# Three rebuilt weight sums fetched from DRAM scratch, row-scale sums on ScalarE, and a new loop order in a two-level seven-product matmul

## The chip, the cores and the metric

The kernel runs on one core of one Trainium2 chip. The metric is the time of one execution in device microseconds (us). Three runs of the kernel before took 1449.6, 1449.54 and 1449.25 us; the median is 1449.54 us. The engines are named PE (TensorE matmul), PEld (its weight loads), DVE (VectorE), ACT (ScalarE), POOL (GpSimd) and SP (SyncE, which here issues every transfer of the steady loop).

## The reference

```python
x: (8, 2048, 2048) float32      w: (2048, 2048) float32
cs   = np.cumsum(x, axis=1)
diff = cs - np.concatenate([zeros, cs[:, :-1, :]], axis=1)
out  = np.matmul(diff, w).astype(np.float32)
```

The difference of a running sum is x again, so the kernel computes out = x w: 16384 rows of 2048, in 128 tiles of 128 rows.

## The kernel before, in words

**Two levels of seven products.** w lies in on-chip memory as float16 in four blocks with the sums T1 to T4 beside them. The first four row tiles are multiplied plainly while w arrives, the next groups have passages of their own, and from then on a loop works through groups of four tiles, called g, h, k, l. The pair (g, k) and the pair (h, l) each are a 2 x 2 block problem, and the outer level needs seven products P1 to P7 for it. P6 and P7 are done whole: four pieces each for g and for h, with four matmuls in a piece (`P6g.0` to `P7h.3`). P1 to P5 join g and h once more into an inner 2 x 2 problem with seven quarter products, `p1` to `p7`, of four matmuls each. So a group has 5 x 7 + 16 = 51 steps of four matmuls, 204 in all, each 128 x 128 by 128 x 512.

**The weight sums.** A quarter product needs a sum of weight quarters. Most are kept. Six have no room and are rebuilt for every group into one buffer, `flow` (128 x 2048 float16, 512 KB): the sums for P1.p4, P2.p4, P3.p2, P4.p4, P5.p5 and P5.p4. Each is one subtraction or addition on DVE (`fill_by`, L955; steps named `P1.fp4` and so on). As `flow` is one buffer, a fill can begin only when the product that read the last content is over. (In the last group P4's sum goes to another buffer.)

**The rows.** A tile of x comes in as two loads of 512 KB (`load`, L113) into the buffer F, which has three places for the first half of a tile and two for the second. ACT sums the absolute values of each half (`weigh0`, `weigh1`, L125); DVE adds the two sums and takes the reciprocal (`scale`, L142 and L144); POOL makes the factors for the way back (`unit`, L150); ACT scales the rows to float16 in place (`narrow0`, `narrow1`, L164); two transfers transpose them (`turn0`, `turn1`, L177). The products go to the eight PSUM banks; ACT copies (`keep`, L636; `P1.cg`, `P5.cg` and the like, L1046) and DVE adds (`add`, L639; L1053) bring them into results of 128 x 512, which SP stores (`put`, L650).

**What sets the order.** `ORDER` is a list of step names written out by hand. A step marked +0 is of one group, +1 of the next, +2 of the one after. The list is gone through once per group, and `after(engine, ...)` makes every instruction of an engine issue after the one before it in this list, so each engine, and SP with its transfers, works strictly in list order: an instruction that waits holds back everything behind it on its engine. Loads, transposes and stores all stand in the one list of SP. `END_ORDER` and `SOONER` reorder the last group. There are 30 groups of this kind; the first of them has its own order for all but P4 and C21.

Of the kernel before, what the change touches and what calls it, by code (L numbers as in the profile page):

```python
# [10 lines left out]
def kernel(  # L11
# [34 lines left out]
    END = M // P  # L46
# [57 lines left out]
    unit = {}  # L104
# [13 lines left out]
    def weigh(t, sides=range(2)):  # L118
        if t < END:
            if t not in sums_of:  # L120
                sums_of[t] = numbers.tile([P, 8], f32, name="of")
            for i in sides:
                after(
                    "act",
                    lambda: nc.scalar.activation(  # L125
                        waste,
                        where[t][i],
                        ABS,
                        scale=1.0 / ROW,
                        accum_out=sums_of[t][:, i : i + 1],  # L130
                    ),
                )

    def scale_of(t):
        if t < END:
            m2 = sums_of.pop(t)
            m, s = (m2[:, i : i + 1] for i in (2, 3))
            u = m2[:, 4:6]
            scales[t], unit[t] = s, u
            after(  # L140
                "dve",
                lambda: nc.vector.tensor_scalar(m, m2[:, :1], m2[:, 1:2], TINY, ADD, MAX),  # L142
            )
            after("dve", lambda: nc.vector.reciprocal(s, m))  # L144
            sizes[t] = m
# [40 lines left out]
    with ExitStack() as head:  # L186
# [195 lines left out]
        for ko in range(1, KO - 1):  # L382
# [3 lines left out]
            q = (ko + 1) // KQ  # L386
# [192 lines left out]
    def in_twos(t):  # L579
        return t if len(t.shape) == 4 else t.rearrange("p (a b) n -> p a b n", b=2)  # L580
# [371 lines left out]
    def fill_by(op, a, b):  # L952
        def some(to):
            x, y = (in_twos(t) for t in (a, b))
            after("dve", lambda: nc.vector.tensor_tensor(in_twos(to), x, y, op))  # L955

        return some

    sevens = {
        "P1": (in_1, {"p4": fill_by(SUB, quarter_of(0, 1, 0), S1_all)}),  # L960
        "P2": (in_2, {"p4": fill_by(SUB, quarter_of(4, 1, 0), inner[:, 8:12, :])}),
        "P3": (in_3, {"p2": fill_by(ADD, spare_of(2, 0), inner[:, 16:20, :])}),
        "P4": (in_4, {"p4": fill_by(SUB, quarter_of(7, 1, 0), spare_of(2, 4))}),
        "P5": (
            in_5,
            {
# [6 lines left out]
    scratch = list(passing)  # L973

    class Group:
        def __init__(self, g):
            self.tiles = dict(g=g, h=g + 2, k=g + 1, l=g + 3)
            self.last = g + 4 == END
            self.at = {}
            self.do = {}  # L980
            self.sums = {}
            self.plan()
# [57 lines left out]
                p1=a[0], p2=a[1], p3=to[4], p4=b[1], p5=to[1], p6=to[2], p7=to[3]  # L1040
            )

        def copy(self, name, to, pool, b):
            def some():
                c, p = self.take(to, pool), self.at[b]
                after("act", lambda: nc.scalar.copy(c, p))  # L1046
# [24 lines left out]

# [24 lines left out]
        def plan(self):  # L1096
            tiles = self.tiles
            half = {}
# [76 lines left out]
            self.add("C12h1", q, "q")  # L1175
            self.add("C12h0", q, "q", let=True)

            self.whole("P7", T3, half["g"][0], half["h"][0], *x)
            for n, c in zip(x, ("C22h0", "C22h1", "C22g0", "C22g1")):
                self.add(c, n, "x")  # L1180

# [48 lines left out]
                    self.step(f"{P}{c}.{j}", some, a, to, j)  # L1230

    ORDER = """
    put.C12g1+0 turn1.h+1 add.C12h1.q+0 P4.p6+0 P4.p5+0 P1.cg+1 P1.p2+1
    add.C12h0.q+0 put.C12h0+0 P1.s1+1 narrow1.k+1 P4.s4+0 P4.p3+0 turn0.k+1
    keep.C21g1+0 P1.s2+1 P1.s4+1 P1.p5+1 add.C22h0.x+0 P1.ct+1 add.C21h1.e+0
    unit.h+1 P1.p6+1 unit.g+1 add.C21g1.q+0 add.C21g0.x+0 weigh0.l+1 P1.s3+1
    weigh1.l+1 turn1.k+1 P2.cv+1 P4.p4+0 add.C21g1.x+0 put.C12h1+0 put.C21g1+0
    P1.m1+1 P4.p7+0 P1.fp4+1 put.C21g0+0 load.g+2 P2.s1+1 P2.s2+1 P1.p7+1
    P1.m2+1 P2.s4+1 P2.p1+1 P1.p3+1 keep.C11g1+1 S1.g+1 S2.g+1 P1.p4+1
    keep.C11g0+1 add.C21h1.q+0 scale.l+1 unit.l+1 narrow0.l+1 put.C22h0+0  # L1240
    put.C21h1+0 P2.p2+1 add.C11g0.v+1 P6g.0+1 P2.fp4+1 P2.p6+1 turn0.l+1
    narrow1.l+1 turn1.l+1 keep.C11h1+1 P6g.1+1 P2.s3+1 add.C11g1.q+1 unit.k+1
    S4.g+1 P2.p5+1 P6g.3+1 keep.C11h0+1 add.C11h1.e+1 P2.p7+1 keep.C21h0+0
    add.C11h1.q+1 P6g.2+1 weigh0.g+2 load.h+2 add.C21h0.x+0 P5.p1+1 P2.p4+1
    S3.g+1 keep.C12g1+1 P2.p3+1 keep.C12g0+1 add.C11h0.q+1 put.C11h0+1 P5.fp5+1
    weigh1.g+2 S1.h+1 P7g.0+1 P5.s1+1 P7g.1+1 scale.g+2 P5.cg+1 P5.s2+1 P5.s4+1
    put.C21h0+0 narrow0.g+2 narrow1.g+2 S2.h+1 P5.s3+1 P5.p2+1 P5.p5+1 P5.ct+1
    add.C11g1.e+1 P5.fp4+1 P5.p6+1 P5.m1+1 put.C11g0+1 keep.C22g0+1 weigh0.h+2
    weigh1.h+2 S4.h+1 P3.s1+1 put.C11h1+1 P6h.2+1 P6h.1+1 put.C11g1+1 P3.s2+1
    P6h.3+1 P6h.0+1 keep.C12h1+1 P5.p7+1 P5.m2+1 keep.C22h1+1 S3.h+1 P3.s4+1  # L1250
    P3.s3+1 P7g.2+1 P7g.3+1 P5.p4+1 add.C22g0.x+1 P3.fp2+1 P5.p3+1 keep.C12h0+1
    add.C12h1.z+1 P7h.0+1 load.k+2 P3.p2+1 scale.h+2 narrow0.h+2 P3.p1+1 P7h.2+1
    put.C22g0+1 turn0.g+2 turn1.g+2 add.C12g0.z+1 weigh0.k+2 add.C12g0.q+1
    put.C12g0+1 P4.fp4+1 keep.C22g1+1 P7h.1+1 P7h.3+1 add.C22g1.x+1 put.C22g1+1
    P3.p3+1 add.C22h1.x+1 P4.s1+1 P4.s3+1 put.C22h1+1 keep.C22h0+1 P3.p6+1
    P3.p4+1 add.C12g1.q+1 add.C12g1.z+1 turn0.h+2 add.C12h0.z+1 weigh1.k+2
    narrow1.h+2 load.l+2 P3.p5+1 scale.k+2 P4.p2+1 P4.p1+1 keep.C21g0+1
    keep.C21h1+1 P3.p7+1 narrow0.k+2 P1.p1+2 add.C12g1.e+1 add.C12h1.e+1 P4.s2+1
    """
    ORDER = [(s[:-2], int(s[-2:])) for s in ORDER.split()]  # L1260
    early = max(n for _, n in ORDER)
# [26 lines left out]
    for b in range(-early, len(groups) - late):  # L1288
        for name, ahead in ORDER:
            i = b + ahead  # L1290
            if 0 <= i < len(groups) and name in groups[i].do:
                if i == len(groups) - 1 and name in END_ORDER:
                    continue
                if groups[i] is half and name == 'keep.C21h1':
                    continue
                if i == 1 and name in before:
                    before[name]()
                groups[i].do.pop(name)()
                if groups[i] is first and name == 'P1.cg':
# [36 lines left out]
```

## Time and profile before

| | |
|---|---|
| median of three runs | 1449.54 us |
| profiled execution, first to last instruction | 1447.4 us |
| PE busy | 1437.9 us (99%) |
| DVE busy | 1319.0 us (91%) |
| ACT busy | 970.5 us (67%) |
| POOL busy | 43.8 us (3%) |
| transfers' packets, share of 16 DMA engines | 86.5% |
| granted TensorE clock | 1.000 |

The profile describes one execution. For that execution only the span is listed, no time of its own beside it, and the span is 2.1 us less than the median of the runs. Busy shares are means over the whole span; matmuls are pipelined and their ends are modelled. A time "to landing" of a transfer runs from the start of its issue on SP to its completion semaphore.

### The profile page before, as it was taken

What the parts mean: (1) busy time and instruction counts of PE and PEld (TensorE: products, weight loads), DVE (VectorE), ACT (ScalarE), POOL (GpSimd) and SP (SyncE); (2) the same over time, 40 slices, a digit from 0 to 9 for tenths busy, and PEclk for the clock granted to TensorE, in tenths of its full rate; (3) what the DMA queues carried; (4) which work ended last, traced back from release to release, by engine and by line L of the source; (5) the groups of instructions that cost most, each with busy time, mean ns of one, the idle gap of its engine ahead of it and who ended that gap; (6) DMA issues with size and microseconds to landing.
All of it is one profiled execution on the core that took longest, in us unless ns stands there. A gap on an engine that the chain in (4) does not pass through costs nothing.

```text
span 1447.4 us, 20191 instructions
## 1 busy us (share of the span) xinstructions
PE 1437.9 (99%) x6686; PEld 651.6 (45%) x6692; DVE 1319.0 (91%) x2310; ACT 970.5 (67%) x1472; POOL 43.8 (3%) x130
## 2 busy tenths in 40 slices
PE   8999999999999999999999999999999999999998
PEld 4444444444444444444444444444444444444443
DVE  4899899999999999999999999999999999999998
ACT  6987566666666776666666667666667766666662
POOL 0011000000000000000000000000000000000000
PEclk9999999999999999999999999999999999999999
DMA  9999788899888898888899888998878998889973
GB/s 363 368 257 298 200 234 232 239 253 253 226 224 239 238 254 245 231 233 236 248 247 232 234 238 233 262 240 234 228 234 240 252 234 239 226 242 248 255 200 127
DMA packets 378199, 351.58 MB, mean 243 GB/s; under 512 B 274800, under 2 KB 274800, under 8 KB 377968
## 3 DMA queue, kind: packets, MB, share of 16 engines
q1 hardware_dynamic: 378096, 350.31, 86.5%
q8 instruction: 52, 0.85, 0.2%
q14 instruction: 51, 0.42, 0.1%
HBM read 150.99 MB, written 134.22 MB: 197 GB/s over the span
## 4 chain that ended last, share of the span: by engine, by line
PE 97%; DMA 2%; DVE 0%; SPq 0%; issue 0%; DVEq 0%
PE b L628 62%; PE b L609 33%; PE b L304 2%; DMA W<-in_w_dram 2%; DMA W<-in_x_dram 0%; DVE c L639 0%; PE b L464 0%; SPq L225 0%; DVE wb L267 0%; SPq L259 0%; DVEq L267 0%; DVEq L639 0%
## 5 line engine op out<-in xcount | busy, mean ns | idle before, releaser
L639 DVE SCALAR_TENSOR_TENSOR c<-b,of,c 128x512 f32<-128x512 f32 x790 | 573.6, 746 | 71.1 <-PE b L628 61.4
L609 PE MATMUL b<-W,x 128*128 128x512 f16 x2144 | 507.1, 379 | 0.0
L636 ACT ACTIVATE c<-b,of 128x512 f32<-128x512 f32 x492 | 312.7, 680 | 220.2 <-PE b L628 113.8
L628 PE MATMUL b<-W,x 128*128 128x512 f16 x1904 | 454.9, 379 | 0.0
L164 ACT ACTIVATE F<-F,of 128x1024 f16<-128x1024 f32 x246 | 282.3, 1148 | 175.6 <-DVE of L144 173.4
L628 PEld LDWEIGHTS <-x 128*128 128x128 f16 x2500 | 244.6, 98 | 295.4 <-issue 1.0
L609 PEld LDWEIGHTS <-x 128*128 128x128 f16 x2144 | 209.7, 98 | 253.3 <-issue 0.5
L125 ACT ACTIVATE waste<-F 128x1024 uint8<-128x1024 f32 x246 | 259.3, 1054 | 8.3 <-DMA F<-in_x_dram 6.2
L628 PEld LDWEIGHTS <-inner 128*128 128x128 f16 x1644 | 160.8, 98 | 194.0
L628 PE MATMUL b<-W,inner 128*128 128x512 f16 x940 | 241.2, 379 | 0.0
L599 DVE TENSOR_TENSOR x<-x,x 128x1024 f16<-128x1024 f16 (+1 forms) x390 | 227.1, 583 | 3.3
L628 PE MATMUL b<-flow,x 128*128 128x512 f16 x584 | 149.9, 379 | 0.0
L628 PE MATMUL b<-inner 128*128 128x512 f16 x472 | 121.1, 379 | 0.0
L955 DVE TENSOR_TENSOR flow<-W 128x2048 f16<-128x2048 f16 x87 | 105.7, 1215 | 0.0
L1053 DVE TENSOR_TENSOR b<-b,c 128x512 f32<-128x512 f32 x116 | 80.4, 693 | 12.7 <-PE b L628 12.7
L150 POOL TENSOR_SCALAR of<-uw,of 128x2 f32<-128x2 f32 x124 | 42.6, 357 | 1299.6 <-DVE of L142 717.1
L955 DVE TENSOR_TENSOR flow<-W,inner 128x2048 f16<-128x2048 f16 x58 | 70.7, 1220 | 0.0
L1046 ACT COPY c<-b 128x512 f32<-128x512 f32 x58 | 33.4, 576 | 51.2 <-PE b L628 51.2
L304 PE MATMUL b<-wb,xP 128*128 128x512 bf16 x234 | 53.2, 379 | 2.2 <-ACT wb L265 1.1
L599 DVE TENSOR_TENSOR inner<-x 128x512 f16<-128x512 f16 x117 | 49.3, 421 | 3.1 <-DMA x<-F 1.0
L1046 ACT COPY b<-b 128x512 f32<-128x512 f32 x87 | 51.2, 589 | 0.2 <-PE b L628 0.2
L599 DVE TENSOR_TENSOR inner<-x,inner 128x512 f16<-128x512 f16 x117 | 49.2, 421 | 2.0
(68 smaller groups left out, 517.5 us busy)
## 6 DMA issues: line engine op xcount, KB each, us to landing
F<-in_x_dram SPq DMA_DIRECT2D x246, 512.0 KB, 5.2
out_dram<-c SPq DMA_DIRECT2D x492, 256.0 KB, 3.0
W<-in_w_dram SPq DMA_DIRECT2D x32, 512.0 KB, 8.4
W<-in_x_dram SPq DMA_DIRECT2D x16, 256.0 KB, 7.8
x<-F SPq DMA_TRANSPOSE x246, 3.4
out_dram<-o SPq DMA_DIRECT2D x5, 256.0 KB, 7.0
out_dram<-wb SPq DMA_DIRECT2D x5, 256.0 KB, 7.0
xP<-in_x_dram SPq DMA_DIRECT2D x1, 1024.0 KB, 6.4
```

The lines of the kernel that those rows point to most:

```text
L125: lambda: nc.scalar.activation(waste, where[t][i], ABS, scale=1.0 / ROW, accum_out=sums_of[t][:, i : i + 1],),
L150: after("pool", lambda: nc.gpsimd.tensor_scalar(u, uw, m, None, MUL))
L164: lambda: nc.scalar.activation(narrowed(t)[:, ds(i * NH, NH)], where[t][i], COPY, scale=s),
L304: lambda: nc.tensor.matmul(ps[r][n], xP[:, r, ko, :], wb[h, ko][:, ds(n * NB, NB)], start=(ko == 0), stop=(ko == KO - 1),),
L599: after("dve", lambda: nc.vector.tensor_tensor(dst.all, p.all, q.all, op))
L609: said = nc.tensor.matmul(to[n], a[k], b[k][:, n, :], start=(first and k == 0), stop=(k == KH - 1), skip_group_check=True,)
L628: said = nc.tensor.matmul(to, a[k], b[k], start=(first and k == 0), stop=(k == 3), skip_group_check=True)
L636: after("act", lambda: nc.scalar.activation(c, p, COPY, scale=u))
L639: after("dve", lambda: nc.vector.scalar_tensor_tensor(c, p, u, c, MUL, ADD))
L955: after("dve", lambda: nc.vector.tensor_tensor(in_twos(to), x, y, op))
L1046: after("act", lambda: nc.scalar.copy(c, p))
L1053: after("dve", lambda: nc.vector.tensor_tensor(t, p, s, ADD))
```

## The change

Four things are edited.

1. `kept_from` wraps three of the six fills: P1.fp4, P3.fp2 and P4.fp4. The first time, the DVE instruction fills the buffer as before, and SP stores the 512 KB to a DRAM tile. Every later time SP fetches the 512 KB from that tile into the buffer, and DVE does nothing. The other three fills stay on DVE.
2. The two absolute sums of a row are added on ACT (`activation` Identity with the second sum as bias) instead of on DVE (L142). The guard against zero, which was a maximum in the DVE instruction, becomes a bias of TINY / 2048 in each element of the absolute sum (L125). The reciprocal stays on DVE.
3. `ORDER` is a new permutation of the same 188 steps.
4. `Group` takes a flag `fine` with a new method `seven_more`, which would do P7 by seven quarter products. Every group is made with `fine` False, so nothing of it is issued. `SOONER` skips a step that is already done.

```diff
                         ABS,
+                        bias=TINY / D,
                         scale=1.0 / ROW,
...
             after(
-                "dve",
-                lambda: nc.vector.tensor_scalar(m, m2[:, :1], m2[:, 1:2], TINY, ADD, MAX),
+                "act",
+                lambda: nc.scalar.activation(m, m2[:, :1], IDENTITY, bias=m2[:, 1:2]),
             )
             after("dve", lambda: nc.vector.reciprocal(s, m))
...
+    kept = ctx.enter_context(
+        tc.tile_pool(name="kept", bufs=1, space=bass.MemoryType.DRAM)
+    )
+
+    def kept_from(make, name):
+        home = kept.tile([P, 4 * NB], f16, name=name)
+        known = []
+
+        def some(to):
+            flat = in_twos(to).rearrange("p a b n -> p (a b n)")
+            if known:
+                after("sp", lambda: nc.sync.dma_start(flat, home))
+            else:
+                make(to)
+                after("sp", lambda: nc.sync.dma_start(home, flat))
+                known.append(True)
+
+        return some
+
     sevens = {
-        "P1": (in_1, {"p4": fill_by(SUB, quarter_of(0, 1, 0), S1_all)}),
+        "P1": (in_1, {"p4": kept_from(fill_by(SUB, quarter_of(0, 1, 0), S1_all), "P1p4")}),
         "P2": (in_2, {"p4": fill_by(SUB, quarter_of(4, 1, 0), inner[:, 8:12, :])}),
-        "P3": (in_3, {"p2": fill_by(ADD, spare_of(2, 0), inner[:, 16:20, :])}),
-        "P4": (in_4, {"p4": fill_by(SUB, quarter_of(7, 1, 0), spare_of(2, 4))}),
+        "P3": (in_3, {"p2": kept_from(fill_by(ADD, spare_of(2, 0), inner[:, 16:20, :]), "P3p2")}),
+        "P4": (in_4, {"p4": kept_from(fill_by(SUB, quarter_of(7, 1, 0), spare_of(2, 4)), "P4p4")}),
...
-            self.whole("P7", T3, half["g"][0], half["h"][0], *x)
+            if self.fine:
+                self.small_sums("P7", A("g", 0), A("h", 0), True, {2: A("l", 0)[0]})
+                self.seven_more("P7", *x)
+            else:
+                self.whole("P7", T3, half["g"][0], half["h"][0], *x)
...
     ORDER = """
-    put.C12g1+0 turn1.h+1 add.C12h1.q+0 P4.p6+0 P4.p5+0 P1.cg+1 P1.p2+1
...
-    unit.h+1 P1.p6+1 unit.g+1 add.C21g1.q+0 add.C21g0.x+0 weigh0.l+1 P1.s3+1
-    weigh1.l+1 turn1.k+1 P2.cv+1 P4.p4+0 add.C21g1.x+0 put.C12h1+0 put.C21g1+0
-    P1.m1+1 P4.p7+0 P1.fp4+1 put.C21g0+0 load.g+2 P2.s1+1 P2.s2+1 P1.p7+1
-    P1.m2+1 P2.s4+1 P2.p1+1 P1.p3+1 keep.C11g1+1 S1.g+1 S2.g+1 P1.p4+1
...
-    P3.s3+1 P7g.2+1 P7g.3+1 P5.p4+1 add.C22g0.x+1 P3.fp2+1 P5.p3+1 keep.C12h0+1
-    add.C12h1.z+1 P7h.0+1 load.k+2 P3.p2+1 scale.h+2 narrow0.h+2 P3.p1+1 P7h.2+1
...
+    unit.h+1 P1.s1+1 P4.s4+0 P4.p5+0 add.C22h0.x+0 add.C21g0.x+0 P1.cg+1
+    turn1.h+1 P4.p6+0 put.C12g1+0 weigh0.l+1 keep.C21g1+0 P1.s3+1 P1.s2+1
+    P1.s4+1 narrow1.k+1 put.C22h0+0 turn1.k+1 weigh1.l+1 add.C21g1.q+0 P1.p2+1
+    add.C21h1.e+0 put.C21g0+0 P4.p3+0 P1.p6+1 P2.cv+1 add.C12h1.q+0
+    add.C12h0.q+0 turn0.k+1 add.C21g1.x+0 put.C21g1+0 P4.p7+0 P1.p5+1 P2.s1+1
+    add.C21h1.q+0 P2.p1+1 P1.ct+1 P4.p4+0 P1.m1+1 scale.l+1 P1.fp4+1 P1.p7+1
+    P2.s2+1 unit.g+1 narrow0.l+1 P2.p2+1 keep.C21h0+0 P1.p3+1 P2.p5+1 S1.g+1
+    put.C12h1+0 keep.C11g0+1 narrow1.l+1 turn0.l+1 keep.C11g1+1 P1.m2+1 P2.s3+1
+    S2.g+1 P2.s4+1 P2.p6+1 turn1.l+1 put.C12h0+0 keep.C11h1+1 P1.p4+1 P6g.2+1
+    add.C11g1.q+1 add.C21h0.x+0 add.C11h1.e+1 P2.fp4+1 P2.p7+1 load.g+2 P6g.1+1
+    S1.h+1 unit.k+1 P6g.3+1 P5.s1+1 P2.p3+1 add.C11h1.q+1 P6g.0+1 add.C11g0.v+1
+    keep.C11h0+1 S2.h+1 P2.p4+1 P5.p1+1 P6h.2+1 put.C11g0+1 weigh0.g+2 P5.fp5+1
+    add.C11g1.e+1 weigh1.g+2 P5.s2+1 unit.l+1 put.C21h0+0 P5.s3+1 P5.s4+1
+    P5.p5+1 S4.g+1 P6h.0+1 S3.g+1 load.h+2 keep.C12g0+1 P5.cg+1 put.C21h1+0
+    scale.g+2 P5.p2+1 P5.ct+1 S4.h+1 P5.p6+1 keep.C12g1+1 P7g.1+1 add.C11h0.q+1
+    P5.m1+1 P6h.3+1 narrow0.g+2 put.C11g1+1 P3.s1+1 P5.p7+1 P5.fp4+1 P7g.0+1
+    P4.s1+1 weigh0.h+2 P6h.1+1 weigh1.h+2 P5.m2+1 narrow1.g+2 P3.s2+1
+    put.C11h0+1 P5.p4+1 put.C11h1+1 P5.p3+1 scale.h+2 load.k+2 keep.C22g0+1
+    P7g.2+1 keep.C22h1+1 S3.h+1 keep.C12h1+1 add.C12h1.z+1 P7g.3+1 P3.p1+1
+    add.C22g0.x+1 P3.s4+1 keep.C12h0+1 P4.s2+1 add.C12g0.q+1 P7h.3+1 narrow0.h+2
+    P3.fp2+1 P3.p2+1 P7h.0+1 turn0.g+2 put.C22g0+1 weigh1.k+2 keep.C22g1+1
+    P7h.2+1 P3.s3+1 keep.C22h0+1 P7h.1+1 P3.p4+1 add.C22g1.x+1 weigh0.k+2
+    add.C12g0.z+1 P3.p6+1 turn1.g+2 put.C12g0+1 scale.k+2 P3.p3+1 put.C22g1+1
+    turn0.h+2 add.C12h0.z+1 P4.s3+1 narrow1.h+2 add.C22h1.x+1 add.C12g1.q+1
+    P4.p1+1 P3.p5+1 load.l+2 add.C12g1.z+1 add.C12g1.e+1 narrow0.k+2 put.C22h1+1
+    add.C12h1.e+1 P3.p7+1 P4.p2+1 keep.C21g0+1 P1.p1+2 keep.C21h1+1 P4.fp4+1
     """
...
-    groups = [Group(g) for g in range(PLAIN + 4, END, 4)]
+    groups = [Group(g, False) for g in range(PLAIN + 4, END, 4)]
...
                 for sooner in SOONER.get(name, ()) if i == len(groups) - 1 else ():
-                    groups[i].do.pop(sooner)()
+                    if sooner in groups[i].do:
+                        groups[i].do.pop(sooner)()
```

More of the change, by code (lines that the diff above doesn't have):

```diff
@@ L37 @@
     ABS = mybir.ActivationFunctionType.Abs
+    IDENTITY = mybir.ActivationFunctionType.Identity
     TOP = 2048.0
@@ L975, with __init__ @@
     class Group:
-        def __init__(self, g):
+        def __init__(self, g, fine):
             self.tiles = dict(g=g, h=g + 2, k=g + 1, l=g + 3)
             self.last = g + 4 == END
+            self.fine = fine
             self.at = {}
@@ L1041, in small_sums, with copy @@
             )
-        def copy(self, name, to, pool, b):
+        def copy(self, name, to, pool, b, let=False):
             def some():
@@ L1046, in some @@
                 after("act", lambda: nc.scalar.copy(c, p))
+                self.close(b, let)
             self.step(name, some)
@@ L1068, in by_seven, with seven_more, into @@
             self.merge(f"{P}.m2", h1, h0, f"{P}t", let=True)
+            self.quarter(P, "p3", g1, False)
+            self.quarter(P, "p4", h0, False)
+        def seven_more(self, P, h0, h1, g0, g1):
+            q, e = f"{P}q", f"{P}e"
+            def into(to, c, i, let=False):
+                self.merge(f"{P}.m{i}", to, to, c, let=let)
+            self.quarter(P, "p1", q, True)
+            self.copy(f"{P}.c1", "7a", free, q)
+            into(g0, "7a", 1, True)
+            self.quarter(P, "p6", q, False)
+            self.copy(f"{P}.c2", "7b", free, q)
+            into(g1, "7b", 2, True)
+            self.quarter(P, "p7", q, False)
+            self.copy(f"{P}.c3", "7c", free, q, let=True)
+            into(h0, "7c", 3)
+            into(h1, "7c", 4, True)
+            self.quarter(P, "p5", e, True)
+            self.copy(f"{P}.c4", "7d", free, e, let=True)
+            into(g1, "7d", 5)
+            into(h1, "7d", 6, True)
+            self.quarter(P, "p2", g0, False)
             self.quarter(P, "p3", g1, False)
@@ L1232 @@
     ORDER = """
-    put.C12g1+0 turn1.h+1 add.C12h1.q+0 P4.p6+0 P4.p5+0 P1.cg+1 P1.p2+1
-    add.C12h0.q+0 put.C12h0+0 P1.s1+1 narrow1.k+1 P4.s4+0 P4.p3+0 turn0.k+1
-    keep.C21g1+0 P1.s2+1 P1.s4+1 P1.p5+1 add.C22h0.x+0 P1.ct+1 add.C21h1.e+0
-    unit.h+1 P1.p6+1 unit.g+1 add.C21g1.q+0 add.C21g0.x+0 weigh0.l+1 P1.s3+1
-    weigh1.l+1 turn1.k+1 P2.cv+1 P4.p4+0 add.C21g1.x+0 put.C12h1+0 put.C21g1+0
-    P1.m1+1 P4.p7+0 P1.fp4+1 put.C21g0+0 load.g+2 P2.s1+1 P2.s2+1 P1.p7+1
-    P1.m2+1 P2.s4+1 P2.p1+1 P1.p3+1 keep.C11g1+1 S1.g+1 S2.g+1 P1.p4+1
@@ L1240 @@
[L1240 to L1250, printed above, removed]
-    P3.s3+1 P7g.2+1 P7g.3+1 P5.p4+1 add.C22g0.x+1 P3.fp2+1 P5.p3+1 keep.C12h0+1
-    add.C12h1.z+1 P7h.0+1 load.k+2 P3.p2+1 scale.h+2 narrow0.h+2 P3.p1+1 P7h.2+1
-    put.C22g0+1 turn0.g+2 turn1.g+2 add.C12g0.z+1 weigh0.k+2 add.C12g0.q+1
@@ L1254 @@
[L1254 to L1258, printed above, removed]
+    unit.h+1 P1.s1+1 P4.s4+0 P4.p5+0 add.C22h0.x+0 add.C21g0.x+0 P1.cg+1
+    turn1.h+1 P4.p6+0 put.C12g1+0 weigh0.l+1 keep.C21g1+0 P1.s3+1 P1.s2+1
```

## The prediction

> **What bounds the kernel now.** I read the page first, then the waits of PE, then the chain that ended last, then one group of the loop, and at last the transfers.
>
> ```profile
> span 1447.4 us, 20191 instructions
> ...
> PE 1437.9 (99%) x6686; PEld 651.6 (45%) x6692; DVE 1319.0 (91%) x2310; ACT 970.5 (67%) x1472; POOL 43.8 (3%) x130
> ...
> PEclk9999999999999999999999999999999999999999
> ...
> q1 hardware_dynamic: 378096, 350.31, 86.5%
> ```
>
> PE is busy for 99% of the span at full clock. Busy alone proves little, since the ends of matmuls are modelled, so the waits of PE come next (waited for, total us, times, longest).
>
> ```profile
> PE b L244 <- DVE W L235: 1.6, 3, 0.6
> PE b L353 <- DVE F L207: 1.2, 1, 1.2
> PE b L304 <- ACT wb L265: 1.1, 1, 1.1
> PE b L304 <- DVE wb L267: 0.7, 1, 0.7
> ```
>
> These are all of them, 4.6 us, and every line is of the start, where w arrives. The matmuls of the loop (L609 and L628) never wait. The chain that ended last, in order of time (start, us, what), says the same: the same piece comes back at a fixed distance.
>
> ```profile
> 25.27 7.82 DMA W<-in_w_dram
> ...
> 375.64 18.13 PE b L628 x84
> ...
> 419.67 18.13 PE b L628 x84
> ...
> 1432.36 7.06 PE b L628 x32
> ```
>
> 419.67 - 375.64 = 44.03 us is one group. In that stretch (columns: PE, PEld, DVE, ACT, POOL busy with counts, clock, share of the DMA engines, GB/s) and in a stretch of the start that only loads:
>
> ```profile
> 9.00:25.00 16.00, 15.41 (x96) 7.39 (x97) 8.33 (x12) 12.96 (x20) 0.00 (x0) 1.00 1.04 404
> 375.64:419.67 44.03, 44.03 (x205) 19.95 (x204) 40.80 (x72) 29.61 (x46) 1.09 (x4) 1.00 0.88 241
> ```
>
> PE has 204 matmuls in 44.03 us, 0.2158 us each, and no gap. A step of four matmuls is 0.863 us. So DVE at 40.80 of 44.03 us is full but not late, and **nothing that only unloads DVE can shorten a group**. Any wait that the change puts in front of a matmul lengthens it by its full size. What is left to gain is the start (loads of w until 33 us, which the change does not touch) and the tail behind the last matmul.
>
> **The change part by part.**
>
> *The fills taken from DVE.* The fills are these groups (shapes, count, busy us, mean ns, idle before):
>
> ```profile
> L955 DVE TENSOR_TENSOR flow<-W 128x2048 f16<-128x2048 f16 x87 | 105.7, 1215 | 0.0
> L955 DVE TENSOR_TENSOR flow<-W,inner 128x2048 f16<-128x2048 f16 x58 | 70.7, 1220 | 0.0
> L955 DVE TENSOR_TENSOR flow<-W,S 128x2048 f16<-128x2048 f16 x29 | 35.2, 1215 | 0.0
> ```
>
> P1's sum is the third row, made 29 times; P3's is half of the second row, 29; P4's is made 30 times (29 of the first row and one into another buffer). One of each stays on DVE, so 28 + 28 + 29 = 85 fills go, 85 x 1.217 = 103 us of DVE, or 3 x 1.217 = 3.65 us a group. All of it lies beside PE: worth 0.
>
> *What comes in their place.* 85 fetches of 512 KB on SP's list, and three stores. In the stretch of loads above the engines moved 404 GB/s at full share, so 524288 bytes take 1.30 us of all 16 engines, 3.9 us a group: the DMA share goes from 0.88 to 0.88 + 3.9 / 44.03 = 0.97. That still fits, but a fetch will often find work ahead of it.
>
> What decides is one distance. `flow` is one buffer, so a fetch can be issued only when the product before has read it, and the next product waits for its landing. Counted in the new order: between P4.p4 and P1.p4 stand P1.p7, P2.p2, P1.p3, P2.p5, P2.p6; between P5.p4 and P3.p2 stand P5.p3, P7g.2, P7g.3, P3.p1, P7h.3. **Five steps each, 5 x 0.863 = 4.32 us.** Before, four and two steps were enough for a DVE instruction of 1.22 us. The third, from P3.p2 to P4.p4, has 19 steps or 16.4 us, and is safe. So PE waits (landing - 4.32 us) at two places of every group, whenever that is above zero.
>
> The nearest rows for the landing are the loads of x, of the same 512 KB in the same 4 KB lines, over 200 issues of the loop, and then two of them by themselves: a pair issued with one small store ahead of it, and one issued right behind two transposes.
>
> ```profile
> L113 SPq DMA_DIRECT2D F<-in_x_dram x200: 343/432/1994, 257.2 to 1347.8; - x100
> ...
> DMA to landing us min/median/max: 3.9/5.1/7.2
> ```
>
> ```profile
> L113 SPq DMA_DIRECT2D F<-in_x_dram x2: 397/414/431, 892.1 to 892.6; - x2
> ...
> DMA to landing us min/median/max: 3.9/4.4/4.9
> ```
>
> ```profile
> L113 SPq DMA_DIRECT2D F<-in_x_dram x1: 717/717/717, 882.4 to 882.4; - x1
> ...
> DMA to landing us min/median/max: 5.4/5.4/5.4
> ```
>
> So 3.9 us when the queue is quiet (that is also the least of 200), 4.9 as second of a pair, 5.4 behind two transposes. The distance of 4.32 lies between them: each place costs between 0 and 1.1 us.
>
> *P1.* Ahead of P1.fp4 on SP stand turn1.k, put.C21g0, turn0.k and put.C21g1.
>
> ```profile
> L164 ACT ACTIVATE F<-F,of 128x1024 f16<-128x1024 f32 x246 | 282.3, 1148 | 175.6 <-DVE of L144 173.4
> L125 ACT ACTIVATE waste<-F 128x1024 uint8<-128x1024 f32 x246 | 259.3, 1054 | 8.3 <-DMA F<-in_x_dram 6.2
> L636 ACT ACTIVATE c<-b,of 128x512 f32<-128x512 f32 x492 | 312.7, 680 | 220.2 <-PE b L628 113.8
> L1046 ACT COPY b<-b 128x512 f32<-128x512 f32 x87 | 51.2, 589 | 0.2 <-PE b L628 0.2
> ...
> L125 ACT ACTIVATION_READ_ACCUMULATOR waste<-F 128x1 f32 x246 | 47.5, 193 | 0.0
> ```
>
> turn1.k waits for narrow1.k, which on ACT follows P1.cg, weigh0.l and keep.C21g1: 0.59 + 1.05 + 0.19 + 0.68 + 1.15 = 3.7 us after the list's start. SP issues a transpose in 1.3 us (row below), so turn0.k goes out near 5.4 and put.C21g1 near 7 us; P4.p4 ends after nine steps, 7.8 us. The transposes are then mostly over but not quite. I take 4.6, between quiet and behind two transposes, nearer to quiet: 0.3 us of wait.
>
> ```profile
> L177 SPq DMA_TRANSPOSE x<-F x200: 1230/1280/2648, 249.6 to 1345.6; - x100
> ...
> DMA to landing us min/median/max: 3.0/3.3/6.1
> ```
>
> *P3.* Ahead of P3.fp2 stands load.k+2, two more loads, whose second half may overwrite its place only after narrow1.g+2 on ACT. Its chain on DVE:
>
> ```profile
> L639 DVE SCALAR_TENSOR_TENSOR c<-b,of,c 128x512 f32<-128x512 f32 x790 | 573.6, 746 | 71.1 <-PE b L628 61.4
> ...
> L599 DVE TENSOR_TENSOR inner<-x 128x512 f16<-128x512 f16 x117 | 49.3, 421 | 3.1 <-DMA x<-F 1.0
> ...
> L599 DVE TENSOR_TENSOR x<-S,x 128x1024 f16<-128x1024 f16 x4 | 2.8, 690 | 0.2
> ```
>
> P2.p4 ends after 22 steps, 19.0 us; then come P5.fp5, add.C11g1.e, P5.s2, s3, s4, S4.g, S3.g and the reciprocal of g: 1.22 + 0.75 + 3 x 0.42 + 2 x 0.69 + 0.16 = 4.8, so 23.8 us. On ACT narrow0.g, weigh0.h, weigh1.h and narrow1.g follow: 2 x 1.15 + 2 x 1.25 = 4.8, so narrow1.g+2 ends about 28.6 us into the list, P5.p4 after 34 steps at 29.3. So the load is issued some 0.8 us before the fetch. In the pair of rows above the second landed 0.5 + 4.9 - 3.9 = 1.5 us behind the first, so the fetch lands 3.9 - 0.8 + 1.5 = 4.6 us after its issue: 0.3 us of wait. While SP waits for the `flow` reader, turn0.g+2 and the puts stand behind it; they wait for products later than that anyway.
>
> *The row scales.* Per tile a DVE instruction (205 ns) becomes an ACT one.
>
> ```profile
> L142 DVE TENSOR_SCALAR of<-of 128x1 f32<-128x1 f32 x124 | 25.4, 205 | 4.4 <-ACT waste L125 4.3
> L144 DVE RECIPROCAL of<-of 128x1 f32<-128x1 f32 x124 | 20.3, 164 | 4.3
> ...
> L265 ACT ACT_TABLE_LOAD x1 | 1.3, 1283 | 0.7 <-PEq L1320 0.7
> ```
>
> No row has Identity on 128 x 1. Below it stands the accumulator read, 0.19 us; above it the copy of 512 columns, 0.59 us. I take 0.25, near the small one: 1 us a group. The bias on the absolute sums costs nothing or, if it is read as a column as L164 reads its scale, 1148 - 1054 = 0.09 us, 0.75 us a group. ACT goes from 29.6 to at most 31.4 of 44.03 us: 0. The upper bound is a table load before and after each Identity, 2 x 1.283 x 4 = 10.3 us a group on ACT, which would make narrow1.g late and lead into the third case below. The row shows one load for Abs and Copy together. The Trainium skill (ScalarE: Activation LUTs, Table sets) says that identity, abs and copy are in every set; by it the load does not happen; no run here shows Identity yet.
>
> *The order and the rest.* The new list moves about everything, but each group still has 204 matmuls and less DVE work; I cost it at 0, covered by DVE's 40.80 - 3.65 - 0.82 = 36.3 of 44.03 us. `fine` is False, so P7 stays whole: 0. Three stores once: under 1 us.
>
> The tail keeps its own order. After the last piece of PE there (start, us, what) the sums of DVE end it:
>
> ```profile
> 1439.51 1.42 DVE c L639 x2
> ...
> 1441.02 1.97 DVE c L639 x3
> ...
> 1443.03 0.75 DVE c L639
> ```
>
> The last add waits for the last product, so less DVE work ahead of it can win a few tenths of a us, not 2.9.
>
> **Sum.** 28 groups x (0.3 + 0.3) = 16.8 us. On the profiled execution: 1447.4 + 16.8 = 1464.2. The median lies 2.1 us above that span; I add it: **1466 us**.
>
> **The rivals.**
>
> *In time at both places.* The queue drains before both fetches, because the freed DVE sends the stores off sooner and SP is idle while it waits for PE. It decides from a landing of 4.32 us down; the least row, 3.9, and its like do it. Then PE waits 0 and the time is 1449.5. For it: 3.9 us behind one store, and no transpose directly ahead of either fetch. Against it: the median of 5.1 and a share of 0.97. The Trainium skill (DMA: Bandwidth & Descriptors, Anatomy of one DMA) gives 2.0 us plus the bytes at 436 GB/s. That would be an estimate of 3.2 us here and this rival; the trace has no load of this size under 3.9.
>
> *The fetch held behind load.k+2.* If narrow1.g+2 ends 1.5 us after P5.p4 instead of before it, the load goes out 1.5 us late, the fetch 0.5 behind it, and lands 1.5 + 0.5 + 4.9 = 6.9 us after the release: 2.6 us of wait, with P1 behind its transposes (5.1 - 4.32 = 0.8) 3.4 us a group, 28 x 3.4 = 95 us: 1545. For it: a chain of load, two weighings, scale and narrow must fit between; every late load of x feeds it. Against: ACT has 12 us a group to spare. Its milder half ends near 1500.
>
> *Shorter.* The tail's adds start less behind: 1446.
>
> **How the numbers follow.** Mild waits 0.45 (own range 1453 to 1490); in time 0.29; held 0.21; shorter 0.05. A difference of 0.2%, 2.9 us, is about what a measurement of this kernel can tell from none. Slower is the first and third, 0.66; the same 0.29; faster 0.05. The range takes in the in-time case below and reaches up to both places at 1.1 us (56 x 1.1 = 61 us, 1511): 1448 to 1510; the worse half of the held case and the shorter one are left out.
>
> **What would show it.** L955 falls from 174 instructions to about 89, L142 disappears, and 85 fetches of `flow` stand among the issues with landings of 3.9 to 5.4 us. Right: PE waits, under L628, for DMA of `flow`, some 56 times, 0.3 us on average, and a group is about 44.6 us. In time: no such line, 44.03 us. Held: SP waits of L113 for ACT just ahead of the fetch, waits of PE over 2 us. The prediction is wrong if PE waits for something else (DVE or ACT by the new order), or if the third fetch, with 16.4 us, is late.

## The result and the profile after

The changed kernel takes 1528.4 us (median of four runs, 1526.5 to 1538.9) against 1449.5 us: a ratio of 1.0559, 95% interval 1.0538 to 1.0579. It is slower, as forecast, but by 79 us and not by 17, and it lies outside the range of 1448 to 1510. The profiled execution took 1528.1 us with a span of 1526.4 us, 79.0 us more than the span before.

The page of the changed kernel (lines of code have moved by some: L609, L628, L639, L955 and L1046 before are L611, L630, L641, L957 and L1068 now; L972 is the fetch):

```profile
span 1526.4 us, 20395 instructions
...
PE 1453.6 (95%) x6686; PEld 649.5 (43%) x6692; DVE 1190.7 (78%) x2101; ACT 996.7 (65%) x1596; POOL 54.9 (4%) x130
...
q1 hardware_dynamic: 390768, 396.45, 95.5%
...
L630 PE MATMUL b<-flow,x 128*128 128x512 f16 x584 | 150.1, 379 | 55.0 <-DMA flow<-P3p 31.6
...
F<-in_x_dram SPq DMA_DIRECT2D x246, 512.0 KB, 5.7
out_dram<-c SPq DMA_DIRECT2D x492, 256.0 KB, 4.1
...
flow<-P4p SPq DMA_DIRECT2D x28, 512.0 KB, 6.8
flow<-P1p SPq DMA_DIRECT2D x28, 512.0 KB, 4.8
flow<-P3p SPq DMA_DIRECT2D x28, 512.0 KB, 5.2
...
x<-F SPq DMA_TRANSPOSE x246, 3.9
```

DVE is 128 us less busy and PE is idle for 73 us, 55 of them ahead of the matmuls that read `flow`. The other transfers land later too: a load of x after 5.7 us (before 5.2), a store after 4.1 (3.0). The waits of PE (waited for, total us, times, longest), which before were all of the start:

```profile
PE b L630 <- DMA flow<-P3p: 31.6, 27, 3.0
PE b L630 <- DVE c L641: 11.1, 10, 1.9
PE b L630 <- DMA flow<-P1p: 9.9, 12, 1.9
PE b L630 <- ACT b L1068: 3.7, 7, 0.7
PE b L630 <- ACT c L638: 3.0, 2, 2.6
```

The second row is credited to a DVE add. But eight of its ten waits stand at P1.p4, where the fetch of P1 had landed 0.14 us before the matmul started; only the other two, at P2.p4, are of DVE.

To see where the time went I took the starts of all matmuls in the trace and counted four to a step. Whatever two starts are further apart than 0.216 us is lost at that step. The sum agrees with the growth of the span in every kernel below (us lost from 150 us into the span to its end; columns are steps of the list; the loop's first P3.p2, whose sum DVE makes in every kernel, is under "other"):

```
kernel                    P1.p4  P3.p2  P1.p7  P5.p2  P3.p4  P4.p7,P2.p1  P2.p4  P5.p5  other    sum   span less 1447.4
before                      0      0      0      0      0         0         0      0     0.2     0.2      -
changed                    25.5   36.2    2.0    5.9    3.3       0.4       1.8    0     4.5    79.6    79.0
e1 fills on DVE             0     44.6   13.0    5.1    0         2.4       0      0     3.8    68.9    68.2
e2 P4 alone                 0     44.6    8.3    6.8    0         2.7       0      0     3.0    65.4    65.2
e3 P1 alone                20.4   44.9   13.4    2.0    0         4.9       0.4    0     3.9    89.9    89.6
e4 P3 alone                 0     37.9   13.3    5.7    4.2       4.7       0      0     5.2    71.0    71.0
e5 e1, fill moved           0      0     14.0    7.5    5.0       3.2       0      0     2.3    32.0    31.4
e12 list alone              0      0     13.8    7.2    4.1       3.4       0      0     2.5    31.0    31.1
e9 e5, two moves            0.1    0      0      0      4.3       5.1       0.1   11.7   3.3    24.6    24.2
e6 eight steps              0      0.4   15.4    5.1   27.3      31.3      18.2    0    13.4   111.1   110.6
e7 sums on before           0      0      0      0      0         0         0      0     0.3     0.3    -0.1
e8 P4 on before             0      0      0.5    0      0         0         0      0     0.6     1.1     1.6
e10 all on before         102.3   53.9    4.6    0      0         0         0      0    65.0   225.8   226.2
e11 copies beside           0      0      0.4    0      0.6       0         0      0.9   8.6    10.5    11.3
```

So of 79.6 us the two fetches with five steps hold 61.7; the rest, 18 us, stands elsewhere. Of it 1.6 us are the loop's first P3.p2, where PE waits for DVE's fill.

### The profile page after: what moved, and what is told of

Same layout as the page of the kernel before. It is cut to its first block, busy times and chain, and to the rows that moved or that the text cites. A ratio compares the mean times of both kernels' runs of the same rounds, so it can differ in the third digit from the quotient of the medians.

```text
span 1526.4 us, 20395 instructions
## 1 busy us (share of the span) xinstructions
PE 1453.6 (95%) x6686; PEld 649.5 (43%) x6692; DVE 1190.7 (78%) x2101; ACT 996.7 (65%) x1596; POOL 54.9 (4%) x130
## 3 DMA queue, kind: packets, MB, share of 16 engines
q1 hardware_dynamic: 390768, 396.45, 95.5%
## 4 chain that ended last, share of the span: by engine, by line
PE 66%; DMA 20%; DVE 7%; issue 3%; ACT 3%; SPq 0%; DVEq 0%; ACTq 0%
PE b L630 42%; PE b L611 23%; DMA flow<-P3p 9%; DMA x<-F 4%; DVE c L641 4%; DMA out_dram<-c 3%; DMA flow<-P1p 2%; DMA W<-in_w_dram 2%; DVE x L601 1%; DVE flow L957 1%; ACT c L638 1%; ACT waste L126 1%; DVE inner L601 1%; ACT F L166 1%; ACT b L1068 1%
## 5 line engine op out<-in xcount | busy, mean ns | idle before, releaser
L641 DVE SCALAR_TENSOR_TENSOR c<-b,of,c 128x512 f32<-128x512 f32 x790 | 565.0, 746 | 146.1 <-ACT c L638 66.9
L611 PE MATMUL b<-W,x 128*128 128x512 f16 x2144 | 512.8, 380 | 0.3 <-DVE x L601 0.3
L630 PE MATMUL b<-W,x 128*128 128x512 f16 x1904 | 459.3, 379 | 7.4 <-ACT b L1068 3.7
L630 PEld LDWEIGHTS <-x 128*128 128x128 f16 x2500 | 242.2, 98 | 372.5 <-issue 90.1
L611 PEld LDWEIGHTS <-x 128*128 128x128 f16 x2144 | 210.0, 98 | 254.8 <-issue 2.2
L166 ACT ACTIVATE F<-F,of 128x1024 f16<-128x1024 f32 x246 | 278.3, 1142 | 32.2 <-DVE of L146 31.7
L630 PEld LDWEIGHTS <-inner 128*128 128x128 f16 x1644 | 160.7, 98 | 196.4 <-issue 2.7
L630 PE MATMUL b<-W,inner 128*128 128x512 f16 x940 | 241.2, 379 | 1.2 <-DVE of L146 0.7
L630 PE MATMUL b<-flow,x 128*128 128x512 f16 x584 | 150.1, 379 | 55.0 <-DMA flow<-P3p 31.6
L630 PE MATMUL b<-inner 128*128 128x512 f16 x472 | 116.4, 379 | 0.0
L152 POOL TENSOR_SCALAR of<-uw,of 128x2 f32<-128x2 f32 x124 | 53.7, 444 | 1362.5 <-ACT of L144 669.5
L1068 ACT COPY b<-b 128x512 f32<-128x512 f32 x87 | 50.5, 581 | 66.9 <-PE b L630 63.8
L146 DVE RECIPROCAL of<-of 128x1 f32<-128x1 f32 x124 | 19.8, 159 | 86.4 <-ACT of L144 86.0
L957 DVE TENSOR_TENSOR flow<-W 128x2048 f16<-128x2048 f16 x59 | 72.1, 1221 | 15.9 <-PE b L630 15.9
L1068 ACT COPY c<-b 128x512 f32<-128x512 f32 x58 | 33.5, 578 | 31.5 <-PE b L630 31.5
```

Source lines behind the costliest of these rows:

```text
L152: after("pool", lambda: nc.gpsimd.tensor_scalar(u, uw, m, None, MUL))
L166: lambda: nc.scalar.activation(narrowed(t)[:, ds(i * NH, NH)], where[t][i], COPY, scale=s),
L611: said = nc.tensor.matmul(to[n], a[k], b[k][:, n, :], start=(first and k == 0), stop=(k == KH - 1), skip_group_check=True,)
L630: said = nc.tensor.matmul(to, a[k], b[k], start=(first and k == 0), stop=(k == 3), skip_group_check=True)
L641: after("dve", lambda: nc.vector.scalar_tensor_tensor(c, p, u, c, MUL, ADD))
```

## The experiments

Theory A after the result: each of the two fetches lands later than its distance, and PE pays the difference. Rival B: 44 MB more fill the queues and everything is late. Rival O: the new order or the sums on ACT cost time by themselves.

**e1 to e4: the fetches undone one by one.**

```diff
-  "P1": (in_1, {"p4": kept_from(fill_by(SUB, quarter_of(0, 1, 0), S1_all), "P1p4")}),
+  "P1": (in_1, {"p4": fill_by(SUB, quarter_of(0, 1, 0), S1_all)}),
   (e1: so for P1, P3 and P4; e2: P1 and P3; e3: P3 and P4; e4: P1 and P4)
```

> The changed kernel with all three fills back on DVE: new order and ScalarE sums stay, no fetch. In the changed kernel 61.5 us of its 79 us stand at the two products that wait for a fetch (25.5 at P1.p4, 36.0 at P3.p2), 17.8 us at other places. Theory A (each of the two fetches lands later than the 4.15 us between its two products, and PE pays the difference): 1449.5 us, within 2. Rival O (the new order or the sums on ScalarE cost time by themselves): the 17.8 us stay, 1467 us. Rival B (the 44 MB more fill the transfer queues and all else comes late): 1449.5 us too.

> The changed kernel with only P4's sum fetched, which has 19 steps (16.4 us) to land; P1 and P3 filled on DVE. Theory A: no wait of PE, 1449.5 us, within 2. Rival B: a third of the added bytes costs a third of the 79 us, about 1476 us.

> Only P1's sum fetched. Theory A: 28 waits of landing less 4.15 us; with fewer transfers ahead landings of 4.3 to 4.8 us, waits of 0.3 to 0.8 us, 1458 to 1472 us. Rival B: 1476 us, with waits spread over other places than P1.p4.

> Only P3's sum fetched, behind the loads of load.k+2. Theory A: landings near 5 us, 28 waits of 0.6 to 1.2 us, 1466 to 1483 us, all at P3.p2, and e3 and e4 together account for at least 50 of the 79 us. Rival B: 1476 us, spread over other places.

| | us | ratio to before | interval |
|---|---|---|---|
| e1 | 1518.1 | 1.0474 | 1.0458 to 1.0489 |
| e2 | 1513.6 | 1.0442 | 1.0427 to 1.0458 |
| e3 | 1540.9 | 1.0628 | 1.0612 to 1.0644 |
| e4 | 1517.7 | 1.0456 | 1.0435 to 1.0477 |

All four missed what theory A gave, and what the rivals gave too. e1 has no fetch and is still 69 us slower, so theory A alone cannot be the cause. But e1 turned out not to be a clean removal. Its waits of PE:

```profile
PE b L630 <- DVE flow L957: 41.5, 29, 1.4
PE b L630 <- DVE of L146: 7.3, 24, 0.4
PE b L630 <- ACT b L1068: 3.1, 6, 0.8
```

In the new list P3.fp2 stands right ahead of P3.p2, behind an add of P3.p1. SP comes to it in time, DVE does not: the fill ends 1.6 us late in every group. In e1, e2 and e3 these 45 us take the place of the 36 of the fetch. What does hold is the table's split: P1's fetch alone loses 20.4 us at P1.p4 (e3), P3's alone 37.9 us at P3.p2 (e4), and P4's nothing. e2 is even 4.5 us faster than e1, and 4.7 us less are lost at P1.p7: in this order, unlike the old one, less work on DVE does help. And P1.p7 loses 13 us in e1 with no fetch at all.

**e5 and e12: the list without fetches.** In e5 the fill of P3 is moved up; in e12 the sums go back to DVE as well, so that only the list is new.

```diff
-  ... keep.C22h1+1 S3.h+1 keep.C12h1+1 ... narrow0.h+2 P3.fp2+1 P3.p2+1 ...
+  ... keep.C22h1+1 S3.h+1 P3.fp2+1 keep.C12h1+1 ... narrow0.h+2 P3.p2+1 ...
   (e12 also has L142's DVE sum again, and no bias)
```

> All three fills on DVE as in e1, and P3.fp2 moved up in the list to behind S3.h, since in e1 DVE reached it 1.6 us too late 28 times (44.6 us at P3.p2). What is left is the new order and the ScalarE sums. Theory O2 (the new order itself costs about 20 us, at P1.p7, where 28 waits of 0.46 us stood in e1, and at P5.p2): P3.p2 loses nothing, 1449.5 + 13 + 5 + 5 = 1472 us, 1468 to 1476. Rival: these waits too came from the late P3.p2, 1449.5 us.

> e5 with the row-scale sums back on DVE too: of the change only the new list is left (and P3.fp2 moved up in it). Theory O2 (the list alone costs what e5 lost): 1478 to 1484 us, with P1.p7 near 14 us and P5.p2 near 7 us again. Rival (the sums on ScalarE, free in the old order, are what makes P1.p7 and P5.p2 late in the new one): 1470 us or less.

e5: 1480.7 us, ratio 1.021 (1.0195 to 1.0225). e12: 1481.4 us, 1.0226 (1.0209 to 1.0243). The new list, with this one fill moved up in it, costs 32 us by itself, and the sums make no difference to it. In e12's waits of PE the two places stand out:

```profile
PE b L629 <- DVE b L1075: 10.2, 30, 0.5
PE b L629 <- ACT b L1067: 5.1, 10, 0.9
PE b L629 <- ACT c L637: 2.8, 5, 0.7
```

The first is P1.p7. It writes the bank that the merge P1.m1 (L1075) reads, and P1.m1 needs the copy P1.ct (L1067) of P1.p5. The new list has two steps between P1.p5 and P1.p7 where the old had three. Here is one such place in time (start, us; DVE, ACT and PE rows are of three answers):

```profile
259.20 0.58 ACT L1067 COPY c<-b 128x512 f32<-128x512 f32 x1 [0.20 <-PE b L629]
```

```profile
256.47 3.38 DVE L640 SCALAR_TENSOR_TENSOR c<-b,of,c 128x512 f32<-128x512 f32 x5 [0.25 <-ACT c L637]
259.77 0.41 DVE L600 TENSOR_TENSOR inner<-x 128x512 f16<-128x512 f16 x1
260.10 0.74 DVE L640 SCALAR_TENSOR_TENSOR c<-b,of,c 128x512 f32<-128x512 f32 x1
260.77 0.69 DVE L1075 TENSOR_TENSOR b<-b,c 128x512 f32<-128x512 f32 x1
```

```profile
260.11 1.03 PE L629 MATMUL b<-flow,x 128*128 128x512 f16 x4
261.51 0.81 PE L629 MATMUL b<-W,inner 128*128 128x512 f16 x3 [0.37 <-DVE b L1075]
```

The copy is done at 259.8, but DVE, strictly in list order, has seven instructions ahead of the merge, the last of them add.C21h1.q, and does them without a pause from 256.47 on. So the merge starts at 260.77, 1.0 us after its copy, and ends at 261.46; P1.p7 could have started at 260.97. It loses 0.5 us, in each of 28 groups. The second is P5.p2, which waits for the copy P5.cg. ACT has two weighings of g+2 ahead of it, and their loads come late:

```profile
273.28 1.06 ACT L126 ACTIVATE waste<-F 128x1024 uint8<-128x1024 f32 x1 [5.71 <-DMA F<-in_x_dram]
274.61 1.06 ACT L126 ACTIVATE waste<-F 128x1024 uint8<-128x1024 f32 x1 [0.17 <-DMA F<-in_x_dram]
...
276.23 0.59 ACT L1067 COPY b<-b 128x512 f32<-128x512 f32 x1
```

**e9: mending these two.**

```diff
-  ... P1.fp4+1 P1.p7+1 P2.s2+1 unit.g+1 narrow0.l+1 P2.p2+1 ...
+  ... P1.fp4+1 P2.s2+1 unit.g+1 narrow0.l+1 P2.p2+1 P1.p7+1 ...
-  ... weigh1.g+2 ... keep.C12g0+1 P5.cg+1 put.C21h1+0 ...
+  ... keep.C12g0+1 P5.cg+1 weigh1.g+2 ... put.C21h1+0 ...
```

> e5 (new order, no fetch, 1480.7 us) with two moves in the list: P1.p7 one step later, behind P2.p2, since it lost 14.0 us waiting for the merge P1.m1; and keep.C12g0 and P5.cg ahead of weigh1.g+2 on ScalarE, since P5.p2 lost 7.5 us waiting for P5.cg behind a weighing whose load had not landed. Theory O2 (the order's cost is these short chains): 1480.7 - 21.5 = 1459 us, 1455 to 1467. Rival (the waits are a sign of the whole list being late, and move on to other steps): above 1473 us.

1473.4 us, ratio 1.0163 (1.0148 to 1.0178): 7 us won, not 21, at the edge of the rival. Both waits are gone, as meant, but P5.p5 now loses 11.7 us, 28 times 0.42, where it lost nothing. So the two waits are real, but no single one of them is the list's price: the list has several places with hardly any slack, and mending one shows the next.

**e7: the sums by themselves, on the old order.**

```diff
+                        bias=TINY / D,
...
-                "dve",
-                lambda: nc.vector.tensor_scalar(m, m2[:, :1], m2[:, 1:2], TINY, ADD, MAX),
+                "act",
+                lambda: nc.scalar.activation(m, m2[:, :1], IDENTITY, bias=m2[:, 1:2]),
```

> The kernel before with its own order and fills; only the row-scale sums go to ScalarE (0.29 us each in the changed kernel's trace) and the guard becomes a bias. Theory: ACT has room, 1449.5 us, within 2. Rival (the sums stand in the way of ACT's copies and are part of the order's 18 us): 1455 us or more.

1450.0 us, ratio 1.0002 (0.9992 to 1.0011). The sums are free. One takes 0.29 us on ACT, and no table load joins the one at the start.

**e8: P4's fetch by itself, on the old order.**

```diff
-  "P4": (in_4, {"p4": fill_by(SUB, quarter_of(7, 1, 0), spare_of(2, 4))}),
+  "P4": (in_4, {"p4": kept_from(fill_by(SUB, quarter_of(7, 1, 0), spare_of(2, 4)), "P4p4")}),
```

> The kernel before with its own order; only P4's sum is kept in DRAM and fetched, 18 steps (15.5 us) before its use. Theory A: 1449.5 us, within 2, with 28 or 29 fetches and no wait of PE on them. Rival B: 15 MB more in the queues, 1455 us or more.

1450.6 us, ratio 1.0004 (0.9995 to 1.0013): a fetch with 18 steps to land is free, and DVE's relief is worth nothing in the old order.

**e10: all three fetches on the old order, which had no wait.** The same edit for P1, P3 and P4; the distances are four and two steps.

> The kernel before with its own order, in which PE waits for nothing, and all three sums fetched. The distances are four steps for P1 (3.45 us less 0.16 = 3.29) and two for P3 (1.73 less 0.16 = 1.56). Theory A (landing less distance, nothing else): P1 lands after 4.2 to 4.9 us and P3 after 4.0 to 5.2 us, with 0.1 us to the matmul, so 1.0 to 1.7 and 2.5 to 3.7 us a group, 28 groups: 98 to 151 us, 1548 to 1601 us, all at P1.p4 and P3.p2. Rival B (the bytes in the queues): as in the changed kernel, 1520 to 1535 us, spread over other places.

1675.2 us, ratio 1.1564 (1.1537 to 1.1592): more than theory A gave, and far from rival B. The waits of PE:

```profile
PE b L628 <- DMA flow<-P1p: 88.9, 28, 4.9
PE b L628 <- DMA flow<-P3p: 48.4, 28, 2.1
PE b L628 <- ACT c L636: 17.6, 28, 3.5
```

The formula holds at both places, and the waits there, 93.5 and 53 us, even add up to what theory A gave (98 to 151 us). That is luck, since its inputs were guessed badly: one place was taken too short, the other too long. P3's fetch landed in 3.3 us, less than any load of x before: 3.34 - 1.56 + 0.07 = 1.85 us, and 1.85 was measured (medians). P1's landed in 4.7 us but was issued 1.6 us late, because SP was still at what stands ahead of it: 1.64 + 4.73 + 0.14 - 3.29 = 3.2, measured 3.1. The table's 102.3 us at P1.p4 hold 93.5 of waiting; 42 us, there and in the steps behind it, come from a slower clock (last section), and 19 us from P3.p3, which waits for a copy on ACT. Ahead of that copy ACT had waited for a load of x every time, so here late transfers reach PE by a path that is not the fetch itself.

**e6: three more steps for both fetches in the changed kernel.**

```diff
-  ... P1.p4+1 P6g.2+1 ... add.C11h1.e+1 P2.fp4+1 P2.p7+1 load.g+2 P6g.1+1 S1.h+1 ...
+  ... P6g.2+1 ... add.C11h1.e+1 P2.p7+1 load.g+2 P6g.1+1 P1.p4+1 P2.fp4+1 S1.h+1 ...
-  ... P3.fp2+1 P3.p2+1 P7h.0+1 ... P7h.1+1 P3.p4+1 ...
+  ... P3.fp2+1 P7h.0+1 ... P7h.1+1 P3.p2+1 P3.p4+1 ...
```

> The changed kernel with all three fetches, but P1.p4 and P3.p2 each moved three steps later in the list: eight steps, 6.9 us less the 0.16 by which the matmul's end lags, between release and use. Bytes and fetches stay the same. Theory A (latency over a short distance): the 61.5 us at the two places go, the 18 us of the order stay: 1467 us, 1462 to 1474. Rival B (DMA engines at 95.5% are the bound): little is won, above 1505 us.

1564.4 us, ratio 1.0799 (1.0781 to 1.0817): a miss, slower than the changed kernel. Its fetches and its waits of PE:

```profile
flow<-P1p SPq DMA_DIRECT2D x28, 512.0 KB, 5.1
flow<-P3p SPq DMA_DIRECT2D x28, 512.0 KB, 5.5
```

```profile
PE b L630 <- DVE c L641: 35.7, 52, 1.9
PE b L630 <- ACT c L638: 22.1, 26, 4.0
...
PE b L630 <- DMA flow<-P3p: 0.2, 1, 0.2
```

The fetches land no sooner than before, and PE does not wait for them any more (0.4 us in the table). That half of theory A is shown. But P3.p4, P4.p7 with P2.p1, and P2.p4 now lose 77 us. P2.p4 waits for add.C11h1.q, which stands behind P2.fp4 on DVE, and that fill now waits for the P1.p4 that I moved. P3.p4 waits for a copy on ACT, and ahead of it ACT had waited for a store to land, which frees the copy's buffer, in all 28 groups. One of them (start, us; ACT, then PE, of two answers):

```profile
876.21 0.69 ACT L638 ACTIVATE c<-b,of 128x512 f32<-128x512 f32 x1 [2.00 <-DMA out_dram<-c]
```

```profile
876.95 1.02 PE L630 MATMUL b<-W,x 128*128 128x512 f16 x4 [0.77 <-ACT c L638]
```

In the kernel before ACT waits for a store 1.1 us in all, with the new list and no fetch (e12) 57 us, and in the changed kernel 112 us:

```profile
ACT c L636 <- DMA out_dram<-c: 1.1, 1, 1.1
ACT c L637 <- DMA out_dram<-c: 56.6, 41, 4.1
ACT c L638 <- DMA out_dram<-c: 111.5, 61, 6.6
```

These waits are of ACT and cost nothing by themselves; PE lost 3.3 us behind them at P3.p4 in the changed kernel and 27 here. In this try the order was not mended by moving two products alone.

**e11: the same bytes, with nobody waiting.** The kernel before; beside each of the three DVE fills SP copies 512 KB from one DRAM tile to another.

```diff
+            make(to)
+            if known:
+                after("sp", lambda: nc.sync.dma_start(other, home))
```

> The kernel before with its own order and every sum made by DVE; beside each of the three fills SP also copies the kept 512 KB from one DRAM tile to another, which nothing waits for. So the transfers of the changed kernel's size and number are there without the dependence. Theory A: 1449.5 to 1453 us. Rival B: 1465 us or more, with waits spread over PE's steps.

1460.2 us, ratio 1.0072 (1.0056 to 1.0089): between what the two theories gave, and nearer to B's 1465 than to A's 1453.

```profile
q1 hardware_dynamic: 381248, 396.45, 98.5%
...
F<-in_x_dram SPq DMA_DIRECT2D x246, 512.0 KB, 6.3
...
x<-F SPq DMA_TRANSPOSE x246, 5.2
```

396 MB as in the changed kernel, and a share of 98.5%, above its 95.5%. Transposes land after 5.2 us instead of 3.4, yet PE loses only 10.5 us. So the load on the queues cost about 10 us with the old order, which has slack. A copy inside DRAM is not quite the same load as a fetch, and no run adds these bytes to the new order without the fetches' waits, so rival B's share in the changed kernel stays open.

## Why the prediction was wrong

**Right: the bound.** PE had no gap to give back. e7 and e8 take work from DVE in the old order, and neither is faster.

**Right: the place, and which fetches.** PE waits at P1.p4 and P3.p2, at 27 of 28 fetches each by over 0.1 us, and never for P4's, though that lands last (6.8 us). The 85 fetches, the sums at 0 and the absence of a table load came as said; a sum takes 0.29 us where I took 0.25.

**Wrong by size: 0.3 + 0.3 us a group.** Measured are 0.91 and 1.29 us, 61.7 us in all instead of 16.8. Three inputs were off. The distance was 4.15 us and not 4.32: matmuls follow each other by 0.216 us, but each takes 0.379 (the mean in its row), so the last reader ends 0.163 us after the next step has begun (ends are modelled, but in most groups the fetch goes out 0.03 us after this one). The landing of P1 was 4.84 us (median) and not 4.6, and 0.17 us of handing over come to it: 4.84 + 0.17 - 4.15 = 0.86. At some groups SP came to P1's fetch up to 1 us late. The landing of P3 was 5.24 us (median) and not 4.6; with 0.07 us of handing over that gives 1.16, and a few landings of 6 to 7 us raise the mean to 1.29. One group shows why:

```profile
893.36 2.80 SPq L114 DMA_DIRECT2D F<-in_x_dram  x2
896.58 0.33 SPq L972 DMA_DIRECT2D flow<-P3p  x1
```

and the chain that ended last, over the same stretch (start, us, what):

```profile
895.69 0.88 PE b L630 x4
896.56 0.02 issue
896.58 5.70 DMA flow<-P3p
902.28 0.04 issue
902.32 1.02 PE b L630 x4
```

The second of the two loads went out at 895.82, 0.8 us ahead of the fetch, just as the sum had it. But I gave that load the 3.9 us of a quiet queue. It had the other load of load.k+2 ahead of it, took 5.2 us and landed at 901.0, and the fetch came 1.3 us behind it. My term for "behind a pair" was one transfer too short.

**Wrong in kind: "the order and the rest, I cost it at 0".** This step fails outright: the new list, with P3.fp2 moved up in it, costs 32 us by itself (e12). I covered it with DVE's mean, 36.3 of 44.03 us. A mean is no cover for a stretch without a pause: between P1.p5 and P1.p7 the list gives two steps, 1.73 us less 0.16 for the matmul's end, and the copy P1.ct and the merge P1.m1 would fit with 0.58 + 0.69 us, but DVE came to the merge only 1.0 us after the copy, from seven instructions in a row (4.3 us). I had named the list's wait at the fetches by counting steps and did not do the same for any other product. That PE would wait for DVE or ACT by the new order was among my signs of being wrong, and it came true.

In the changed kernel only 18 us stand outside the two fetches. P1.p7 loses 2.0 us there and 13.8 in e12. A wait for one fetch does not hide this loss, since with P1's or P3's fetch alone it is 13.4 and 13.3 (e3, e4); with P4's sum taken from DVE it is 8.3 (e2). So less work on DVE takes part of it away, and what takes the rest is not shown.

**The rivals.** *In time at both places* came true at one fetch in 56. *Held behind load.k+2* was nearest by its time (1545), but its mechanism did not happen: SP issued P3's fetch within 0.17 us of the reader's end in every group. So the agreement of the time is luck.

What stays open: how the list's 32 us split among its tight places, since e9 showed that they take over from each other; why fewer of them are left in the changed kernel; and how much of the landings of 4.8 and 5.2 us is due to the added bytes and how much to the neighbours in the list.

## What to carry to other kernels

When an engine's work is exchanged for a transfer, what counts is the time between the last reader of the buffer and its next user: hold that against the landing behind the very transfers that stand ahead of it, not against a median, and end it where the matmul ends and not where the next begins. A fetch with 18 steps to land was free here, one with five cost about 1 us every time. Where a hand-made order is new, follow every path from a product through ACT and DVE to the next product in the same bank, with all that stands ahead on each engine, and ask when the stores free the buffers of the copies; a mean of busy time says nothing about these, and to undo a part of such a change its place in the order has to be undone too.

## What the runs showed of the hardware

**In the changed kernel a fetch of 512 KB landed after 3.2 to 7.6 us, by what was ahead.** In e10 the last transfer ahead of P3's fetch goes out some 6 us earlier and has landed when the fetch is issued (in the group at 247.8 us: a store issued at 241.5, landed at 243.9), so the queue is drained:

```profile
flow<-P3p SPq DMA_DIRECT2D x28, 512.0 KB, 3.3
```

In the changed kernel P4's fetch, behind two loads and a store, took 6.8. The 3.9 us that the prediction took for a quiet queue were not quiet. Of the changed kernel's fetches only the last of P3 (3.2) found a drained queue. The Trainium skill (DMA: Bandwidth & Descriptors, Anatomy of one DMA) gives the fit behind the prediction's estimate of 3.2 us, 2.0 us plus the bytes at 436 GB/s, for transfers issued by GpSimd. These go out by SP, and the 3.3 us of e10 agree with it.

**After a long wait the next matmuls can be slow.** In e10 PE was idle for 3.9 us ahead of a P1.p4, and soon after ran at half clock for one stretch (columns as in the windows above: PE busy with count, ..., clock, share, GB/s):

```profile
276.80:280.20 3.40, 3.40 (x10) 1.22 (x8) 0.30 (x1) 2.48 (x5) 0.00 (x0) 0.50 1.13 378
280.20:283.60 3.40, 3.40 (x17) 1.51 (x16) 3.18 (x5) 0.20 (x2) 0.00 (x0) 1.00 1.08 230
```

Ten matmuls in 3.4 us, then seventeen. 22 of its 28 waits for P1's fetch, with PE idle for 2.4 to 4.9 us, were followed by such a stretch, and two of those for P3's; one wait with 3.35 us idle was not. Some 200 matmuls took 0.21 us longer, 42 us together, and e10's mean clock was 0.970. The changed kernel had one such stretch in its loop, after one of its longer waits (2.2 us idle):

```profile
PE b L630 <- DMA flow<-P3p: 27.8, 23, 3.0
```

(its waits between 300 and 1400 us: 23 times, 27.8 us, so 1.2 on average). The Trainium skill (TensorE: Matmul & The Clock Gate, Part 1: The HAM clock gate) says that the clock halves after about one idle window of 3.4 us, the windows running freely. The stretches of 3.4 us agree with that. But PE idle for only 2.0 to 2.2 us was followed by a stretch too (three times, one of them in the changed kernel), which is shorter than the page has it.

**A busy share of 98.5% did not make the transfers the bound.** e11 had it and lost 10.5 us. The share adds up the times of packets and can pass 1: it reads 1.13 and 1.08 in the two stretches above.
